# Column tiles for the adaLN products, rope tables loaded in place, and the output projection's split moved into the z stage of a hybrid backbone kernel

## The chip, the core and the metric

The kernel runs on one core of a Trainium2 chip. The metric is the device time of one execution in microseconds. The core has five engines that run their own instruction streams and meet at semaphores: TensorE (PE, matrix products; its weight loads are shown as PEld), VectorE (DVE), ScalarE (ACT), GpSimd (POOL) and SyncE (SP, which here issues nearly all DMAs). Each takes its instructions in order, so an instruction that waits holds back all that stand behind it on its engine.

## What is computed

Two layers of a diffusion backbone with 2048 latent and 256 context tokens of width 1024. Each layer modulates its input with an adaLN shift and scale, projects it once to 2560 columns, runs three mixers (a gated MLP over chunks of 128 positions, attention with rotary position codes, a recurrent scan), and projects back with w_o:

```python
shift, scale, gate = jnp.split(jax.nn.silu(c) @ w_ada + b_ada, 3, -1)
z = (x * (1 + scale[:, None]) + shift[:, None]) @ w_in
...
q = axial_rope(rms_norm(q.reshape(Bn, L, N_HEADS, HEAD_DIM), q_norm_g), rows, cols)
k = axial_rope(rms_norm(k.reshape(Bn, L, N_KV_HEADS, HEAD_DIM), k_norm_g), rows, cols)
...
attn = blocked_attention(q, jnp.concatenate([k, kc], 1), jnp.concatenate([v, vc], 1))
...
y = jnp.concatenate([mix_a * jax.nn.silu(a_g), attn * jax.nn.silu(b_g),
                     lru * jax.nn.silu(r_g)], -1) @ w_o
x_new = layer_norm(ALPHA * x + gate[:, None] * y, ln_g, ln_b)
```

The context tokens go through the same weights with their own modulation (c_ctx), read only themselves, and are not needed after the second layer's keys, values and scan states.

## The kernel before

**Numbers.** Products that need more than f16 are made of halves: a weight w becomes wh (w in f16, on ACT or POOL) and wl (the rest in f16, on DVE), an input becomes xh and xl, and PE sums xh·wh, xh·wl and xl·wh. One 128x512 split of a weight so costs one ACT and one DVE instruction.

**Stages.** The program starts with the adaLN vectors that layer 0 needs at once (shift and scale); then each layer has a z stage (0 and 1), which makes the projections and all that attention and the scans read, and an attention stage, which makes scores, softmax, the output projection and the layer norm. In the profile z stage 0 lasts to about 694 us, its attention stage to 1540, z stage 1 to 2105, and the second attention stage to the end.

**The z stage** goes over nine blocks of 256 tokens (block 0 is the context). In a block, PE runs sections: cc (the columns of the scan and its gate, transposed, `conv_in`), then the row-wise sections ag, kv, uv and bg, each as two tiles of 128 tokens of 24 matmuls of 512 columns (`nat`, L531 to L533; accumulator zps). The order of PE's instructions is written out by hand: the program is one text in which side work is woven in by `pump`, which advances a generator by a step. The order of the other four engines is set by the tile scheduler from the dependencies, and each of their queues is then fixed.

**adaLN side work.** `ada_rest` is such a generator, advanced by `pump(rest, 1)`, once in each cc product and in each tile of `nat` at k == 4: 12 visits a block from block 1 of layer 0 on. It makes the gates of layer 0 and the whole adaLN vectors of layer 1: eight rows of 512 columns, each a sum over eight chunks of w_ada (128x512, 256 KB, loaded into wga). A visit makes the two products of the chunk whose halves were made before (L376, L377: the stationary operand is vs, 128x4, which holds both halves of both condition vectors; the moving operand is the chunk's half) and then splits the next chunk (ACT L384, DVE L385) into the one buffer wgh. The four rows of the accumulator gtp are summed by a product with sel in `fin`.

**Rope.** For each tile of a latent block `rp` (the cosines and sines of its 128 tokens, 64 KB) is loaded by SP (L605); POOL multiplies it with the norm weights into ct (L607) and sn (L609). DVE multiplies the normed q and k with ct (L614), POOL multiplies the swapped halves with sn into t2 (L620, four instructions a tile), DVE adds (L622) and splits the result into kc and qc (L624 to L630). PE transposes those (kp L642, L643, qp L649), and ACT copies the transposes out to KK, KB and QS (L644, L645, L650). rp, ct, sn, t1 and t2 have one buffer each.

**The attention stage** is ordered by hand on PE, DVE, ACT and POOL, with a running count of each engine's planned time (`use(DV, 0.6)`) by which some steps choose between DVE and POOL; side work advances at set rates. `wo_prep` is its first side work: it loads w_o in eight chunks of 128x1024 and splits them into OH (ACT L915) and OL (DVE L919, two a chunk), and between them loads the gates and norm weights. Scores are sps (L975), their maxima pm (DVE L977), P is the softmax numerator, Pl its low half (L1069, on POOL or DVE); the output projection reads OH and OL at L1179 to L1181.

## Time and profile before

| | before |
|---|---|
| median of 3 runs | 2934.22 us (2933.54 to 2934.83) |
| profiled run | 2931.81 us, span 2929.8 us |
| granted TensorE clock, mean | 0.982 |
| PE, DVE, ACT, POOL busy | 93%, 71%, 48%, 61% of the span |

The profile is one execution of the program. Busy time is the time in which an engine executes; idle time of an engine is given to what it waited for last. A PE row's time includes its pipeline, so that matmuls of 0.38 us start every 0.22 us; costs on PE are therefore read from starts.

### The profile page before, as it was taken

To read this page: it belongs to the slowest core of one execution; us is meant where nothing else is said; L and a number is where in the kernel's file an instruction comes from. 1 tells how busy PE (TensorE), PEld (TensorE's weight loads), DVE (VectorE), ACT (ScalarE), POOL (GpSimd) and SP (SyncE) were. 2 spreads that over 40 slices of the span, in tenths; PEclk is the share of its full clock that TensorE was granted. 3 is DMA by queue.
4 is the path that set the end of the run, shared out by engine and by line. 5 is a ranking of instruction groups with operands and counts; after the bars stand their busy time and mean duration, and the time that the engine had idled before them with its cause. 6 is when DMAs were issued, how large, how long until landed. Compare 5 with 4: busy or idle time off the path is not lost. (4 is left out here: it accounts for less than half of the span.)

```text
span 2929.8 us, 60697 instructions
## 1 busy us (share of the span) xinstructions
PE 2735.1 (93%) x23931; PEld 1820.6 (62%) x23931; DVE 2071.7 (71%) x4102; ACT 1401.6 (48%) x2595; POOL 1782.4 (61%) x1821
## 2 busy tenths in 40 slices
PE   7999999998799999999999899999788999999998
PEld 3544454545677777677765555555466777777775
DVE  8666565558988777777877555554798877777775
ACT  5444444535554445445542454444564544544452
POOL 3233333346888877677764244433597877887775
PEclk9999999999999999999999999999999999999999
DMA  8222222105422110212115111111332210111001
GB/s 291 83 92 92 86 91 78 53 31 174 127 74 64 56 41 27 69 37 70 52 32 160 52 60 50 54 64 42 109 129 95 73 45 24 50 50 42 26 27 44
DMA packets 118255, 213.60 MB, mean 73 GB/s; under 512 B 13873, under 2 KB 45429, under 8 KB 117969
## 3 DMA queue, kind: packets, MB, share of 16 engines
q1 hardware_dynamic: 115620, 208.84, 21.8%
q8 instruction: 187, 3.06, 0.4%
q10 hardware_dynamic: 2348, 0.89, 0.1%
q14 instruction: 100, 0.81, 0.1%
HBM read 147.54 MB, written 62.14 MB: 72 GB/s over the span
## 5 line engine op out<-in xcount | busy, mean ns | idle before, releaser
L1069 POOL TENSOR_TENSOR Pl<-P 128x512 f16<-128x512 f32 x1131 | 1223.7, 1099 | 321.3 <-ACT P L1062 312.9
L1062 ACT ACTIVATE P<-stp 128x512 f32<-128x512 f32 x1160 | 692.4, 597 | 784.1 <-PE stp L1059 699.0
L977 DVE TENSOR_REDUCE pm<-sps 128x1 f32<-128x256 f32 (+1 forms) x1276 | 750.5, 625 | 270.5 <-PE sps L975 267.7
L1059 PE MATMUL stp<-aQB,KB 65*128 65x256 f16 x2320 | 582.5, 276 | 2.8 <-ACT aQB L990 2.8
L1058 PE MATMUL stp<-aQS,KK 128*128 128x256 f16 x2320 | 580.1, 275 | 3.7 <-ACT P L1062 3.2
L1086 PE MATMUL pv<-VX,P 128*128 128x129 f16 x4640 | 560.6, 220 | 0.0
L1088 PE MATMUL pv<-VX,Pl 128*128 128x65 f16 x4640 | 528.5, 193 | 6.4 <-DVE Pl L1069 3.3
L975 PE MATMUL sps<-KK,aQS 128*128 128x256 f16 (+1 forms) x1276 | 458.0, 360 | 62.2 <-DVE pm L977 59.2
L1088 PEld LDWEIGHTS <-Pl 128*128 128x128 f16 x4640 | 416.4, 98 | 99.9 <-POOL Pl L1069 5.0
L1086 PEld LDWEIGHTS <-P 128*128 128x128 bf16 x4640 | 431.1, 98 | 66.3 <-issue 51.4
L1059 PEld LDWEIGHTS <-KB 65*128 65x128 f16 x2320 | 228.7, 99 | 96.4 <-issue 5.8
L1058 PEld LDWEIGHTS <-KK 128*128 128x128 f16 x2320 | 230.6, 99 | 84.2 <-issue 14.5
L520 POOL TENSOR_SCALAR xh<-xm 128x512 f16<-128x512 f32 x68 | 45.9, 674 | 276.9 <-ACT xm L517 276.4
L531 PEld LDWEIGHTS <-xh 128*128 128x128 f16 x1040 | 102.7, 99 | 150.3 <-issue 47.4
L533 PEld LDWEIGHTS <-xl 128*128 128x128 f16 x1040 | 102.9, 99 | 124.6 <-issue 6.2
L532 PEld LDWEIGHTS <-xh 128*128 128x128 f16 x1040 | 102.8, 99 | 108.2 <-issue 4.8
L433 POOL TENSOR_SCALAR gt<-gt,sp 128x256 f32<-128x256 f32 x72 | 41.9, 591 | 199.1 <-ACT gt L430 193.2
L686 PE MATMUL cps<-xl,wh_cc 128*128 128x256 f16 x528 | 147.1, 279 | 2.7 <-DVE xl L521 2.7
L687 PE MATMUL cps<-xh,wl_cc 128*128 128x256 f16 x528 | 147.0, 278 | 1.7 <-DVE wl_cc L185 1.7
L685 PE MATMUL cps<-xh,wh_cc 128*128 128x256 f16 x528 | 147.4, 279 | 0.0
L975 PEld LDWEIGHTS <-aQS 128*128 128x128 f16 x1276 | 125.1, 98 | 11.8 <-issue 0.9
L760 ACT ACTIVATE uv<-uv 128x512 f32<-128x512 f32 x34 | 21.4, 630 | 213.0 <-DVE uv L759 213.0
(285 smaller groups left out, 5586.9 us busy)
## 6 DMA issues: line engine op xcount, KB each, us to landing
wf<-in_w_in_dram SPq DMA_DIRECT2D x64, 256.0 KB
wga<-in_w_ada_dram SPq DMA_DIRECT2D x64, 256.0 KB
lr<-LRd SPq DMA_DIRECT2D x32, 512.0 KB
SBd<-sbg SPq DMA_DIRECT2D x34, 256.0 KB
QSd<-QS SPq DMA_DIRECT2D x17, 512.0 KB
LRd<-gt SPq DMA_DIRECT2D x34, 256.0 KB
aQS<-QSd SPq DMA_DIRECT2D x17, 512.0 KB
asb<-SBd SPq DMA_DIRECT2D x17, 512.0 KB
```

What stands on the lines that cost most here:

```text
L533: T.matmul(ps[:, :w], xl[:, k, ts], wh[:, k, c0:], start=False, stop=(k == KC - 1))
L685: T.matmul(ps, wh[:, k, cs], xh[:, k], start=(k == 0), stop=False)
L686: T.matmul(ps, wh[:, k, cs], xl[:, k], start=False, stop=False)
L687: T.matmul(ps, wl[:, k, cs], xh[:, k], start=False, stop=(k == KC - 1))
L975: T.matmul(ps[:, :w], QS[:, h, t * 128:(t + 1) * 128], KK[:, kv].rearrange("p a b -> p (a b)")[:, k0:k0 + w], start=True, stop=True)
L977: V.tensor_reduce(pm[:, i:i + 1], ps[:, :w], axis=AX, op=OP.max)
L1058: T.matmul(ps[:, i], KK[:, kv, kt], QS[:, h], start=True, stop=False)
L1059: T.matmul(ps[:, i], KB[:, kv, kt], QB[:, h], start=False, stop=True)
L1062: S.activation(P, ps, AF.Exp)
L1069: less_busy(0.6, 1.04, 2.0).tensor_tensor(Pl, P, Ph, op=OP.subtract)
L1086: T.matmul(pv[:, t, 0:129], Ph[:, i, ts], VX[:, kt, kv, 0:129], start=first, stop=False, skip_group_check=True)
L1088: T.matmul(pv[:, t, 64:129], Pl[:, i, ts], VX[:, kt, kv, 64:129], start=False, stop=end, skip_group_check=True)
```

## The change

**Products.** The chunks are taken in pairs. A visit's splits fill half of a wgh of four parts (hi and lo of chunk k, hi and lo of chunk k+1); when both chunks are there, four products go to four groups of rows of one accumulator, rows 0 to 3, 32 to 35, 64 to 67 and 96 to 99, that is to four column positions of the array. The accumulator is first set to zero by a product of zeros over all 128 rows (L394), once in each of the eight sums, and sel (now 128x2) adds all four groups. A pair takes three visits: split, split, and the products with the next pair's first split. The visits stand at k == 1 and k == 5 of each tile of `nat` but the first of uv: 18 a block.

**Output projection.** The 16 tiles (128x512) of w_o of a layer are split in its z stage as further items of `ada_rest`, two visits each, and stored with f16 halves to wo_d in DRAM: in layer 0 between the gates' sums and layer 1's, in layer 1 from its third block on. The attention stage loads OH and OL from wo_d in 16 DMAs.

**Rope.** rp is gone: cosines and sines are loaded straight into ct and sn (each twice, for q's and k's half), and POOL multiplies in place.

```diff
-    sel = cst.tile([4, 2], F32, name="sel")
+    sel = cst.tile([128, 2], F32, name="sel")
...
+    wo_d = [dr.tile([KC, 2, 128, 2, 512], F16, name=f"wo_d{l}") for l in range(DEPTH)]
...
-            V.tensor_tensor(sel, idF[0:4, 0:2], idF[0:4, 2:4], op=OP.add)
+            V.tensor_tensor(sel, idF[:, 0:2], idF[:, 2:4], op=OP.add)
+            for g in range(1, 4):
+                for s in range(2):
+                    V.tensor_tensor(sel, sel, idF[:, 32 * g + 2 * s:32 * g + 2 * s + 2], op=OP.add)
...
+                if l == 0:
+                    todo = [(0, 2, 0), (0, 2, 1), None] + [(a, b, h) for a in range(1, DEPTH) for b in (2, 1, 0) for h in range(2)]
+                else:
+                    todo = [None]
...
+                def split(w):
+                    f = ws.pop(0)
+                    S.activation(w[:, 0], f, AF.Copy, scale=WS)
+                    V.scalar_tensor_tensor(w[:, 1], f, WS, w[:, 0], op0=OP.mult, op1=OP.subtract)
...
-                        if k == 0:
-                            acc = pp.tile([4, 512], F32, name="gtp", tag="zps", bufs=4)
-                        if k == 2:
-                            row = bias(l2, j, h)
-                        T.matmul(acc, vs[:, k], w[:, 0], start=(k == 0), stop=False)
-                        T.matmul(acc, vs[:, k], w[:, 1], start=False, stop=(k == KC - 1))
...
+                            acc = pp.tile([128, 512], F32, name="gtp", tag="zps", bufs=4)
+                            T.matmul(acc, zer, mov, start=True, stop=False, skip_group_check=True)
...
+                        for g in range(4):
+                            T.matmul(acc[32 * g:32 * g + 4], vs[:, k + g // 2], w[:, g], start=False,
+                                     stop=(k == KC - 2), skip_group_check=True)
...
+                        w = zp.tile([128, 2 if l else 4, 512], F16, name="wgh", tag="wgh")
+                        split(w[:, 0:2])
+                        ld(i + 1)
+                        i += 1
+                        yield
+                        if it[0] == "wo":
+                            nc.sync.dma_start(wo_d[l][it[1], it[2]], w[:, 0:2])
+                        else:
+                            split(w[:, 2:4])
                             ld(i + 1)
+                            i += 1
+                            pend = w, it
+                            yield
+                    yield
...
-                    if k == 4:
+                    if side_work and k % 4 == 1:
                         pump(rest, 1)
...
-                        rp = zp.tile([128, 2, 64], F32, name="rp", tag="rp")
-                        nc.sync.dma_start(rp, rope[r0:r0 + 128])
...
-                        G.tensor_tensor(ct, rp[:, 0:1].to_broadcast([128, 2, 64]), K.gqk, op=OP.mult)
...
+                        for a in range(2):
+                            nc.sync.dma_start(ct[:, a], rope[r0:r0 + 128, 0])
+                            nc.sync.dma_start(sn[:, a], rope[r0:r0 + 128, 1])
+                        G.tensor_tensor(ct, ct, K.gqk, op=OP.mult)
+                        G.tensor_tensor(sn, sn, K.gsw.rearrange("p a h s f -> p a (h s f)"), op=OP.mult)
...
-                        ps = nat(xTb, t, "uv")
+                        ps = nat(xTb, t, "uv", 0, t == 1)
...
-                    if l == 0 and bi == 1:
+                    if bi == (2 if last else 1):
                         rest.append(ada_rest())
...
-                    S.activation(OH[:, k], wfs[k], AF.Copy, scale=WS)
-                    yield
-                    for q in range(2):
-                        qs = slice(q * 512, (q + 1) * 512)
-                        V.scalar_tensor_tensor(OL[:, k, qs], wfs[k][:, qs], WS, OH[:, k, qs], op0=OP.mult, op1=OP.subtract)
-                        use(DV, 0.6)
-                        yield
...
+                for hl, o in ((0, OH), (1, OL)):
+                    for k in range(KC):
+                        nc.sync.dma_start(o[:, k].rearrange("p (h n) -> p h n", h=2),
+                                          wo_d[l][k, :, :, hl].rearrange("h p n -> p h n"))
```

The queues change at three places. The rows are instructions in the order in which an engine takes them, outputs left of the arrow; the numbers only tell buffers apart.

PE, block 4 of layer 0, where it takes split weights in the second uv tile; before:

```order
L533 LDWEIGHTS xl_2677
L533 MATMUL zps_3818<-wh_uv_614,xl_2677 128x512
L376 LDWEIGHTS vs_63
L376 MATMUL gtp_3616<-wgh_3800,vs_63 4x512
L377 LDWEIGHTS vs_63
L377 MATMUL gtp_3616<-wgh_3800,vs_63 4x512
L531 LDWEIGHTS xh_2676
L531 MATMUL zps_3818<-wh_uv_614,xh_2676 128x512
```

and after, in the first bg tile:

```order
L563 LDWEIGHTS xl_2662
L563 MATMUL zps_3807<-wh_bg_749,xl_2662 128x512
L400 LDWEIGHTS vs_63
L400 MATMUL gtp_3469<-wgh_3756,vs_63 4x512
L400 LDWEIGHTS vs_63
L400 MATMUL gtp_3469<-wgh_3756,vs_63 4x512
L400 LDWEIGHTS vs_63
L400 MATMUL gtp_3469<-wgh_3756,vs_63 4x512
L400 LDWEIGHTS vs_63
L400 MATMUL gtp_3469<-wgh_3756,vs_63 4x512
L561 LDWEIGHTS xh_2661
L561 MATMUL zps_3807<-wh_bg_749,xh_2661 128x512
```

The visit with products has moved from the second uv tile (after 15 of its matmuls) to the first bg tile (after 18), and has four products, each with its own weight load.

DVE in the same block, from the split that this visit takes (wgh_3800) in the rope step of tile 0 to the next one in that of tile 1; before:

```order
L385 SCALAR_TENSOR_TENSOR wgh_3800<-wga_3679,wgh_3800 128x512
L622 TENSOR_TENSOR t1_3735<-t1_3735,t2_3742 128x640
L759 SCALAR_TENSOR_TENSOR uv_3778<-uv_3778,zps_3779 128x512
L624 CAST kc_3750<-t1_3735 128x2x128
L629 CAST qc_3753<-t1_3735 128x8x64
L625 TENSOR_TENSOR kc_3750<-t1_3735,kc_3750 128x2x64
L630 TENSOR_TENSOR qc_3753<-t1_3735,qc_3753 128x8x64
L614 TENSOR_TENSOR t1_3757<-qk1_3281,ct_3760 128x512
L614 TENSOR_TENSOR t1_3757<-qk1_3281,ct_3760 128x128
L761 SCALAR_TENSOR_TENSOR uv_3778<-uv_3778,zps_3779 128x512
L622 TENSOR_TENSOR t1_3757<-t1_3757,t2_3764 128x640
L385 SCALAR_TENSOR_TENSOR wgh_3836<-wga_3803,wgh_3836 128x512
```

and after, from the rope sum of tile 0 on:

```order
L652 TENSOR_TENSOR t1_3668<-t1_3668,t2_3677 128x640
L789 SCALAR_TENSOR_TENSOR uv_3715<-uv_3715,zps_3716 128x512
L654 CAST kc_3685<-t1_3668 128x2x128
L659 CAST qc_3688<-t1_3668 128x8x64
L655 TENSOR_TENSOR kc_3685<-t1_3668,kc_3685 128x2x64
L660 TENSOR_TENSOR qc_3688<-t1_3668,qc_3688 128x8x64
L365 SCALAR_TENSOR_TENSOR wgh_3756<-wga_3603,wgh_3756 128x512
L644 TENSOR_TENSOR t1_3692<-qk1_3234,ct_3693 128x512
L644 TENSOR_TENSOR t1_3692<-qk1_3234,ct_3693 128x128
L791 SCALAR_TENSOR_TENSOR uv_3715<-uv_3715,zps_3716 128x512
L652 TENSOR_TENSOR t1_3692<-t1_3692,t2_3701 128x640
L365 SCALAR_TENSOR_TENSOR wgh_3756<-wga_3759,wgh_3756 128x512
```

Both splits of the pair (wgh_3756) now stand behind the casts of tile 0, and the second of them behind the rope sum of tile 1 as well (L644 is the former L614, L652 the former L622, L654 to L660 the former L624 to L630, L789 and L791 the former L759 and L761).

POOL, rope step of block 4 of layer 1, from tile 0's products to tile 1's; before:

```order
L620 TENSOR_TENSOR t2_24283<-qk0_23888,sn_24281 128x16x16 x2
L620 TENSOR_TENSOR t2_24283<-qk0_23888,sn_24281 128x4x16 x2
L609 TENSOR_TENSOR sn_24303<-rp_24299,gsw_20295 128x128
L607 TENSOR_TENSOR ct_24301<-rp_24299,gqk_20014 128x128
L620 TENSOR_TENSOR t2_24305<-qk1_23889,sn_24303 128x16x16 x2
L620 TENSOR_TENSOR t2_24305<-qk1_23889,sn_24303 128x4x16 x2
```

and after (L650 is the former L620, L640 the former L609, L639 the former L607):

```order
L650 TENSOR_TENSOR t2_24481<-qk0_24084,sn_24474 128x16x16 x2
L650 TENSOR_TENSOR t2_24481<-qk0_24084,sn_24474 128x4x16 x2
L640 TENSOR_TENSOR sn_24498<-sn_24498,gsw_20386 128x128
L650 TENSOR_TENSOR t2_24505<-qk1_24085,sn_24498 128x16x16 x2
L650 TENSOR_TENSOR t2_24505<-qk1_24085,sn_24498 128x4x16 x2
L639 TENSOR_TENSOR ct_24497<-ct_24497,gqk_20102 128x128
```

sn of tile 1 is multiplied in place, in the buffer that tile 0's products read, and ct of tile 1 stands behind tile 1's products instead of ahead of them.

## Rows read from the trace of the kernel before

**Rows 1.** The page: busy us, share of the span, instructions
```profile
PE 2735.1 (93%) x23931; PEld 1820.6 (62%) x23931; DVE 2071.7 (71%) x4102; ACT 1401.6 (48%) x2595; POOL 1782.4 (61%) x1821
```

**Rows 2.** By stretch: length, busy us (instructions), granted clock, DMA share, GB/s
```profile
39.00:694.00 655.00, 610.33 (x3490) 325.98 (x3491) 404.73 (x750) 303.54 (x555) 238.64 (x274) 0.97 0.28 90
1540.00:2105.00 565.00, 525.72 (x3171) 306.06 (x3170) 338.69 (x619) 249.31 (x467) 223.48 (x265) 0.98 0.21 70
314.00:319.00 5.00, 4.94 (x12) 1.64 (x12) 4.68 (x9) 1.52 (x3) 4.84 (x8) 0.50 0.23 66
722.00:820.00 98.00, 79.28 (x950) 63.21 (x948) 94.85 (x179) 56.66 (x105) 88.27 (x80) 0.97 0.39 121
820.00:920.00 100.00, 95.90 (x1048) 71.58 (x1046) 85.66 (x174) 50.08 (x98) 87.79 (x88) 1.00 0.28 82
2131.00:2230.00 99.00, 78.82 (x941) 63.16 (x939) 95.28 (x176) 57.29 (x105) 86.47 (x79) 0.97 0.37 116
2230.00:2330.00 100.00, 96.90 (x1053) 72.78 (x1053) 84.69 (x173) 49.70 (x96) 86.07 (x87) 0.98 0.23 75
```

**Rows 3.** Tile gtp: duration ns min/median/max, first and last start
```profile
L376 PE MATMUL gtp<-wgh,vs x64: 377/378/379, 116.8 to 508.9; 128*4 128x512 f16 x64
```

**Rows 4.** Timeline of PE, one visit: start us, us, engine, line, operation
```profile
229.22 0.38 PE L532 MATMUL zps<-wl_uv,xh 128*128 128x512 f16 x1
229.44 0.38 PE L533 MATMUL zps<-wh_uv,xl 128*128 128x512 f16 x1
229.75 0.38 PE L376 MATMUL gtp<-wgh,vs 128*4 128x512 f16 x1
229.96 0.38 PE L377 MATMUL gtp<-wgh,vs 128*4 128x512 f16 x1
230.27 0.39 PE L531 MATMUL zps<-wh_uv,xh 128*128 128x512 f16 x1
```

**Rows 5.** Waits by cause, 39 to 694 us: us in total, times, longest
```profile
PE gtp L377 <- DVE wgh L385: 21.4, 5, 5.0
```

**Rows 6.** Timeline of PE, second uv tile of block 4
```profile
309.17 0.38 PE L376 MATMUL gtp<-wgh,vs 128*4 128x512 f16 x1
314.06 0.58 PE L377 MATMUL gtp<-wgh,vs 128*4 128x512 f16 x1 [4.51 <-DVE wgh L385]
```

**Rows 7.** Timeline of POOL, rope products of tile 0 in block 4
```profile
310.75 3.43 POOL L620 TENSOR_TENSOR t<-qk,sn 128x256 f32<-128x256 f32 x4 [0.94 <-DVE qk L596]
```

**Rows 8.** Timeline of DVE, tile 1 of block 4
```profile
322.71 0.67 DVE L385 SCALAR_TENSOR_TENSOR wgh<-wga,wgh 128x512 f16<-128x512 f32 x1
```

**Rows 9.** Timeline of POOL, a plain block of z stage 1
```profile
1885.19 3.06 POOL L620 TENSOR_TENSOR t<-qk,sn 128x256 f32<-128x256 f32 x4 [0.94 <-DVE qk L596]
1888.32 1.09 POOL L609 TENSOR_TENSOR sn<-rp,gsw 128x128 f32<-128x128 f32 x1
1889.38 0.45 POOL L607 TENSOR_TENSOR ct<-rp,gqk 128x128 f32<-128x128 f32 x1
1889.79 2.71 POOL L620 TENSOR_TENSOR t<-qk,sn 128x256 f32<-128x256 f32 x4
```

**Rows 10.** Timeline of DVE in the same block
```profile
1892.42 1.16 DVE L614 TENSOR_TENSOR t<-qk,ct 128x512 f32<-128x512 f32 x2
```

**Rows 11.** Waits by cause, 1540 to 2105 us
```profile
PE kp L642 <- ACT KB L645: 10.2, 7, 5.9
```

**Rows 12.** Timeline of SyncE's queue, head of z stage 1
```profile
1613.21 0.80 SPq L496 DMA_DIRECT2D xn<-x_d  x2
```

**Rows 13.** Timeline of PE at the same place
```profile
1616.65 1.45 PE L514 MATMUL tr<-idF,xn 128*128 128x128 f32 x4 [7.09 <-DMA xn<-x_d]
```

**Rows 14.** Lines of ACT's and DVE's w_o split: duration ns min/median/max
```profile
L915 ACT ACTIVATE OH<-wof x16: 1047/1048/1050, 720.3 to 2213.2; 128x1024 f16<-128x1024 f32 x16
...
L919 DVE SCALAR_TENSOR_TENSOR OL<-wof,OH x32: 678/1242/1529, 722.4 to 2226.8; 128x512 f16<-128x512 f32 x32
```

**Rows 15.** Waits of PE by cause, 694 to 830 us
```profile
PE sps L975 <- DVE pm L977: 15.4, 12, 2.6
```

More of the change, by code (lines that the diff above doesn't have):

```diff
@@ L129, in turn @@
                 for k in range(KC):
-                    T.matmul(tp[:, k], rows[j][:, k // 4, k % 4 * 128:(k % 4 + 1) * 128], sel, start=True, stop=True)
+                    T.matmul(tp[:, k], rows[j][:, k // 4, k % 4 * 128:(k % 4 + 1) * 128], sel[0:4], start=True, stop=True)
                 tps.append(tp)
@@ L333, in ada_rest @@
             def ada_rest():
-                items = [(l2, j, h, k) for l2, j in [(0, 2)] + [(a, b) for a in range(1, DEPTH) for b in (2, 1, 0)]
-                         for h in range(2) for k in range(KC)]
-                ws, parts, acc, row, fins = [], [], None, None, None
+                if l == 0:
+                    todo = [(0, 2, 0), (0, 2, 1), None] + [(a, b, h) for a in range(1, DEPTH) for b in (2, 1, 0) for h in range(2)]
+                else:
+                    todo = [None]
+                items = []
+                for g in todo:
+                    if g is None:
+                        items += [("wo", k, h) for k in range(KC) for h in range(2)]
+                    else:
+                        items += [g + (k,) for k in range(KC)]
+                ws = []
                 def ld(i):
-                    l2, j, h, k = items[i]
+                    if i >= len(items):
+                        return
                     ws.append(zp.tile([128, 512], F32, name="wga", tag="xm", bufs=2))
-                    c0 = j * D + h * 512
-                    nc.sync.dma_start(ws[-1], w_ada[l2, k * 128:(k + 1) * 128, c0:c0 + 512])
-                def bias(l2, j, h):
-                    row = zp.tile([4, 512], F32, name="grow", tag="grow")
-                    V.memset(row, 0.0)
-                    c0 = j * D + h * 512
-                    nc.sync.dma_start(row[0:2], rows_bcast(b_ada[l2, c0:c0 + 512], 512, 2))
-                    return row
+                    if items[i][0] == "wo":
+                        _, k, h = items[i]
+                        src = w_o[l, k * 128:(k + 1) * 128, h * 512:(h + 1) * 512]
+                    else:
+                        l2, j, h, k = items[i]
+                        src = w_ada[l2, k * 128:(k + 1) * 128, j * D + h * 512:j * D + (h + 1) * 512]
+                    nc.sync.dma_start(ws[-1], src)
+                def split(w):
+                    f = ws.pop(0)
+                    S.activation(w[:, 0], f, AF.Copy, scale=WS)
+                    V.scalar_tensor_tensor(w[:, 1], f, WS, w[:, 0], op0=OP.mult, op1=OP.subtract)
                 def fin(l2, j, h, row):
@@ L361, in fin @@
                         nc.sync.dma_start(gate_d[l2][:, h * 512:(h + 1) * 512], row[0:2])
+                zer = MZ[1][:, 0, 0:1].to_broadcast([128, 128])
+                mov = MZ[2][:, 0:1, 0:64].to_broadcast([128, 8, 64])
+                pend, fins, acc, row = None, None, None, None
                 ld(0)
                 yield
-                for i in range(len(items) + 1):
+                i = 0
+                while i < len(items) or pend or fins:
                     if fins:
@@ L381, in ada_rest @@
                     if i < len(items):
[L382 to L387 removed]
+                        it = items[i]
+                        w = zp.tile([128, 2 if l else 4, 512], F16, name="wgh", tag="wgh")
[5 more added lines that the diff above has]
+                            nc.sync.dma_start(wo_d[l][it[1], it[2]], w[:, 0:2])
+                        else:
+                            split(w[:, 2:4])
                             ld(i + 1)
+                            i += 1
+                            pend = w, it
+                            yield
                     yield
[L390 removed]
             W = Wt[l]
@@ L522, in prep, with nat @@
                 xT[b] = (xh, xl)
-            def nat(xT_b, t, g, c0=0):
+            def nat(xT_b, t, g, c0=0, side_work=True):
                 xh, xl = xT_b
```

50 lines of the change are left out of this document (17 added, 33 removed).

## The prediction, made before the changed kernel had run

> **What bounds the kernel now.** I read the busy table first: TensorE (PE) is busy 2735.1 of 2929.8 us [rows 1], so what counts is what PE executes or waits for, and another engine matters only where PE waits for it. The table by stretches says which stage has what limit [rows 2]. In the two z stages PE is busy 93% of the time and VectorE (DVE) about 60%: PE runs the hand-written order there, and short waits break it. The first 98 us of each attention stage in which w_o is split are different: DVE is busy 94.85 of 98 us, PE only 79.28, and 100 us later PE is back at 95.90 of 100. DVE is the bound there. The change touches three places: the adaLN products in z stage 0, the rope step of every z block, and the w_o split.
>
> **Products in column tiles.** Before, 64 chunks take two matmuls each, one visit a chunk (64 first ones in [rows 3]). In the trace of one visit [rows 4] the starts stand 0.31, 0.21 and 0.31 us apart, where neighbours stand 0.22: a visit costs 0.83 − 0.22 = 0.61 us, 64 of them 39.2 us. After, 32 visits have four matmuls each in four column positions, and 8 zeroing matmuls of 0.22 us are new (1.8 us). No row shows column tiles side by side. If they stream beside each other, a visit costs one stream with its two edges, 0.31 + 0.31 − 0.22 = 0.40 us; if in a row, 0.31 + 3 × 0.21 + 0.31 − 0.22 = 1.03 us. I take 0.50, near the first, since the second matmul's weight load of rows 4 did not widen its 0.21 us. That is 16.0 + 1.8 = 17.8 us: **−21.4 us**, ends −24.6 and −4.5.
>
> The 0.31 us edges of rows 4 are what the Trainium skill, TensorEngine Tiling (Array Packing), Tiling Modes, describes: a change of tiling mode drains TensorE. Its page TensorE: Matmul & The Clock Gate, Part 3, says that a pack takes one matmul and about 4 ns for each further tile; an estimate from that is 0.41 us a visit and a sum lower by 3 us. The same part has a rule against this change: a weight load overlaps running matmuls only where its row group differs, and these four have the same rows. By it the four would go in a row, the third rival below; the 0.21 us of rows 4 speaks against it for one column position.
>
> **Waits for the split weights.** Before, PE waited five times, 21.4 us in all, for DVE's half of a chunk [rows 5], 4.51 us of it in the second uv tile of block 4 [rows 6]. In the 5 us behind that wait the granted clock is 0.50, the 1.2 GHz level, and PE makes 12 matmuls [rows 2] that at its usual step of 0.22 us would take 2.6: 2.4 us more. Five times 4.3 + 2.4 is 34 us. The cause is DVE's queue: the split stands behind the rope step, which waits for GpSimd (POOL). After, uv tile 0 has no visit, and the order of DVE puts the pair's second split behind the rope step of tile 1 (blocks 4 to 7 alike); PE wants it in the first bg tile, after 18 of its 24 matmuls. Worked from block 4: POOL ends tile 0's products at 310.75 + 3.43 = 314.2 [rows 7]; only then may the sn load be issued into the one buffer; 1.9 us to land (below), 1.1 for sn, 2.7 for tile 1's products and 0.45 for ct [rows 9], which now stands last, make 320.35; DVE then needs 1.16 for L614 [rows 10], 0.67 for the split [rows 8] and about as much for each of the two rows between: 323.5. PE, at 309.17 after 15 of uv tile 1's matmuls, has 9 + 18 left (5.8 us) and gets there at about 315. The wait is 8.5 us, with the slow matmuls behind it 11. Four blocks make 44, and I allow 5 in block 1, where a pair is only half shifted: 49 for 34, **+15 us**. Ends: −14 if the loads land at once and the waits stay at four of 5 us, +30 if all six blocks with pairs pay 10.5.
>
> **Rope tables.** Before, rp for the next tile lay ready: in a plain block POOL goes from tile 0's products straight to sn, ct and tile 1's products [rows 9]. After, ct and sn are one buffer each and are loaded themselves, so the load of sn for tile 1 waits for POOL's last read of tile 0, and SyncE issues four loads a tile in place of one. In the block of rows 9: products end 1885.19 + 3.06 = 1888.25; landing 1.9 gives 1890.15, sn 1.09 gives 1891.24, products 2.71 give 1893.95, ct 0.45 gives 1894.4. DVE started L614 of tile 1 at 1892.42 [rows 10]; it is **2.0 us later**. Behind it on DVE stand L761 of uv tile 0 and L759 of uv tile 1; ACT's second uv activation (L760) waits for the latter, and ACT's copies KK and KB stand behind that on ACT. PE's kp waits for KB already now, seven times in z stage 1, 10.2 us in all with one of 5.9 [rows 11]: there is no slack, and the 2.0 us go on to PE. The landing time is the unknown: a 256 KB load issued at 1613.21 [rows 12] released PE at 1616.65 [rows 13], so below 3.4 us; two issues of 0.40 each [rows 12] are the least, 0.8. I take 1.9, between them, since a half's load is small (32 KB). The delay is then 2.0, with ends 0.9 and 3.5. Eight blocks of z stage 1: +16 (7 to 28). At its head SyncE's queue has the next block's sn and ct loads ahead of the x load for which PE waits 7.09 us [rows 13]; the ct load waits for DVE's L614 of tile 1, about 1.3 us later than the x load's issue now: +1.3 (0 to 4). In z stage 0 blocks 2, 3 and 8 have no late pair and pay 2.0 each: +6 (3 to 10); in blocks 4 to 7 it is inside the 8.5. Together **+23 us**.
>
> **Output projection.** Before, ACT splits 16 tiles of 1.048 us and DVE 32 of about 1.2 us [rows 14], 17 and 38 us, in the two stretches of rows 2 where DVE is the bound and PE waits for DVE's maxima: 15.4 us in the first [rows 15]. After, the attention stage loads the halves ready-made, 16 loads of 256 KB, as many bytes as before, needed late (the first output projection comes after the first scores). If PE reaches its next level at once, layer 0 gains 98 × (0.959 − 0.809) = 14.7 us and layer 1 99 × (0.969 − 0.796) = 17.1: 32 at best. If DVE fills the room with other due work, the share of the split in its time there (19 of 95) of the 19 and 20 us lost: 8 at least. I take 13 a layer, a little under the 15.4 us of waits: **−26 us**. The 16 splits a layer move to the z stages: 0.67 us each on DVE [rows 8], 11 us in about two blocks, where DVE is 60% busy; PE needs none of their results, so only what stands behind them on DVE pays, and the store, for which the next item's one wgh buffer waits, sits in SyncE's queue. 0 to 6 us, I take **+2**. The six additions for sel at the start are tiny and hidden behind the first loads; the bias load at k = 0 is earlier than before: nothing.
>
> **How the numbers follow.** −21.4 + 15 + 23 − 26 + 2 = −7.4 us on the profiled run's 2931.8: 2924.4. The median of before is 2.4 us above that run, so I say **2927 us** for the median. The ends of the terms do not add up in one direction; about ±13 us around it are likely.
>
> **Rivals.**
> - *The loads are early enough* (chance 0.22). The landing is short, and what PE waited for in rows 11 had another last cause than this chain, so that DVE's delay ends before PE: the rope terms fall to +5, the pair waits stay at 34. −21.4 + 0 + 5 − 26 + 2 = −40: **2893**. For it: DVE is only 60% busy in these stages [rows 2]. Against it: the chain of rows 9 to 11 has no slack, and the buffer is single.
> - *The single buffer costs more than the rest brings* (0.25): slower. Place: sn of tile 1 in every block. At the end of 3.5 us a block, z stage 1 pays 28 + 4, blocks 2, 3 and 8 pay 10, four waits are longer by 1.5 (+21 in place of +15): −21.4 + 21 + 42 − 26 + 2 = +18: **2952**. It decides from about 0.5 us more a block: 15 blocks × 0.5 = 7.5 us cancel the forecast's gain.
> - *The column tiles go in a row* (0.13): 32 × 1.03 + 1.8 = 34.8 for 39.2, the sum +10: **2944**. For it: the page's rule above; against it: rows 4.
> - The forecast, 0.40.
>
> About 0.2% (5.9 us, so 2928.3 and 2940.1) is what a measurement can tell from no change. The forecast lies close to the first of these: I give it 0.24 faster, 0.14 the same, 0.02 slower. The early loads are 0.22 faster; the single buffer 0.05 the same and 0.20 slower; the row of tiles 0.01 faster, 0.04 the same, 0.08 slower. Together 0.47, 0.23 and 0.30. The range, 2888 to 2953, takes in the rivals' centres and leaves out only their far ends; the forecast's own is 2914 to 2940.
>
> **What would show it.** Right: starts within a visit of four matmuls a few hundredths apart; PE's wait for the split weights (now on the four-matmul line) four or five times near 8.5 us in the first bg tile; DVE's L614 of tile 1 (a later line number) waiting for POOL's ct; PE's kp waits in z stage 1 two us longer a block; z stage 0 about as long as now, z stage 1 about 19 us longer, DVE no longer 97% busy at the head of the attention stages and each stage 13 us shorter. Wrong: starts 0.21 us apart (tiles in a row); sn for tile 1 standing on POOL without a gap behind the products (loads early); a rope delay of 3 us or more; or attention stages unchanged because PE was held by the maxima anyway.

## The result: slower by 0.87%

| | before | changed |
|---|---|---|
| median | 2934.15 us (2933.54 to 2934.83) | 2959.61 us (2959.04 to 2961.6) |
| profiled run's span | 2929.8 us | 2957.6 us |
| granted clock, mean | 0.982 | 0.972 |

The ratio is 1.0087 (95% interval 1.0074 to 1.01), +25.5 us; the forecast was 2927. The page's busy table of the changed kernel, beside [rows 1]:

```profile
PE 2729.9 (92%) x23939; PEld 1829.9 (62%) x23939; DVE 2055.8 (70%) x4113; ACT 1400.5 (47%) x2611; POOL 1761.8 (60%) x1816
```

PE is busy 5 us less than before and the span is 28 us longer. By stages, each counted from PE's first cc product of a layer or its first scores to the next such point (start: until layer 0's first cc product; attention 1: until PE's last product):

| us | start | z stage 0 | attention 0 | z stage 1 | attention 1 |
|---|---|---|---|---|---|
| before | 39.5 | 654.4 | 843.2 | 567.6 | 815.9 |
| changed | 41.5 | 670.3 | 839.6 | 593.8 | 803.2 |
| difference | +2.0 | +15.9 | −3.6 | +26.2 | −12.7 |
| forecast | 0 | +1 | −13 | +18 | −13 |

The same view by stretches as [rows 2], of the changed kernel: the z stages, then the heads of the attention stages and the 100 us behind them (length, busy us and instructions by engine, granted clock, DMA share, GB/s):

```profile
41.50:711.80 670.30, 595.59 (x3496) 331.01 (x3494) 405.12 (x765) 307.74 (x570) 232.26 (x272) 0.94 0.31 101
1551.30:2145.10 593.80, 541.21 (x3188) 314.35 (x3187) 336.00 (x641) 259.10 (x484) 218.59 (x267) 0.96 0.25 84
740.00:838.00 98.00, 88.30 (x1072) 70.42 (x1070) 91.23 (x182) 54.90 (x108) 88.94 (x85) 1.00 0.33 107
838.00:938.00 100.00, 92.38 (x995) 68.80 (x992) 87.99 (x168) 47.74 (x93) 85.80 (x86) 0.98 0.25 79
2171.00:2270.00 99.00, 89.24 (x1078) 70.96 (x1075) 92.98 (x186) 55.26 (x108) 90.48 (x86) 1.00 0.34 111
2270.00:2370.00 100.00, 95.42 (x1053) 71.42 (x1052) 84.46 (x168) 49.88 (x96) 87.19 (x87) 1.00 0.21 67
```

z stage 1, which has no adaLN products at all, is the largest loss. The same row for the whole of it before:

```profile
1537.10:2104.70 567.60, 528.32 (x3188) 307.54 (x3186) 340.96 (x624) 250.81 (x468) 224.10 (x266) 0.98 0.21 71
```

Of its 26.2 us, 13.3 are idle time of PE (593.80 − 541.21 for 567.60 − 528.32). The other 12.9 are busy time: PE takes 541.21 us in place of 528.32 for the same 3188 products, since its granted clock fell from 0.98 to 0.96. In z stage 0 the clock fell from 0.97 to 0.94, and PE's idle time grew by 30 us.

At the heads of the attention stages PE is busy 88.30 and 89.24 us where it was 79.28 and 78.82 [rows 2]: 9 and 10 us are gained there. Its wait for the maxima in the first stage's head, 15.4 us in [rows 15], is now:

```profile
PE sps L990 <- DVE pm L992: 8.3, 9, 1.9
```

Layer 1 keeps the gain. Layer 0 does not: in the 100 us behind the head PE is busy 92.38 us, before 95.90. From there to the end of the stage its waits for the maxima are 18.5 us (14.4 before), those for DVE's r, the sum ahead of the layer norm, 5.6 (2.1 before).

**Column tiles.** PE's timeline of one visit, beside [rows 4] (start us, us, engine, line, operation):

```profile
362.22 0.38 PE L562 MATMUL zps<-wl_kv,xh 128*128 128x512 f16 x1
362.44 0.38 PE L563 MATMUL zps<-wh_kv,xl 128*128 128x512 f16 x1
362.75 0.39 PE L400 MATMUL gtp<-wgh,vs 128*4 128x512 f16 x4
363.07 0.39 PE L561 MATMUL zps<-wh_kv,xh 128*128 128x512 f16 x1
```

The four products start 3 to 4 ns apart (x4 in one row), each with a weight load of its own, and take one stream's time: the next full-width matmul starts 0.32 us behind the first of them. The visit costs 0.31 + 0.32 − 0.22 = 0.41 us.

**The rope step.** The block of z stage 1 that answers to [rows 9], on POOL:

```profile
1915.98 3.06 POOL L650 TENSOR_TENSOR t<-qk,sn 128x256 f32<-128x256 f32 x4 [0.94 <-DVE qk L626]
1921.35 0.81 POOL L640 TENSOR_TENSOR sn<-sn,gsw 128x128 f32<-128x128 f32 x1 [2.30 <-DVE kc L655]
1922.24 1.97 POOL L650 TENSOR_TENSOR t<-qk,sn 128x256 f32<-128x256 f32 x4
1924.17 0.46 POOL L639 TENSOR_TENSOR ct<-ct,gqk 128x128 f32<-128x128 f32 x1
```

its loads on SyncE's queue (issues, not landings):

```profile
1919.07 0.81 SPq L638 DMA_DIRECT2D sn<-in_rope_dram  x2
1919.98 0.85 SPq L637 DMA_DIRECT2D ct<-in_rope_dram  x2
```

and DVE's step from tile 0 to tile 1, which stands in [rows 10] for before:

```profile
1921.16 0.68 DVE L660 TENSOR_TENSOR qc<-t,qc 128x512 f16<-128x512 f32 x1
1924.66 0.90 DVE L644 TENSOR_TENSOR t<-qk,ct 128x512 f32<-128x512 f32 x2 [2.81 <-POOL ct L639]
```

POOL ended tile 0's products at 1919.04, SyncE issued sn at once, the multiplication began at 1921.35 when both halves had landed (2.28 us from the first issue), ct came last, and DVE waited 2.81 us for it. The row of the multiplication names DVE's kc, which ended 0.1 us earlier; in the plain blocks it begins 2.2 to 2.5 us behind the first issue, whether kc or the load is named, so the load is what it waits for. All of z stage 1, waits by cause (us in total, times, longest), beside [rows 11]:

```profile
PE kp L672 <- ACT KB L675: 28.7, 7, 9.3
...
POOL sn L640 <- DMA sn<-in_rope_dram: 23.3, 12, 2.6
...
DVE t L644 <- POOL ct L639: 18.7, 7, 2.8
```

PE's wait for KB went from 10.2 to 28.7 us. In a plain block, one without w_o pieces, PE waits 3.4 us in all, before 2.3 us; the block takes 65.2 us for 62.5. The rest of the 2.7 us is the clock. The wait for KB ends the block, and these are the first 5 us of the next one, before and after (behind the length PE's busy time and, in brackets, its matmuls; the granted clock stands third from the end):

```profile
1837.80:1842.80 5.00, 5.00 (x50) 4.47 (x48) 1.55 (x4) 1.80 (x4) 3.73 (x4) 1.00 0.13 52
1867.10:1872.10 5.00, 5.00 (x35) 3.86 (x33) 1.50 (x4) 1.84 (x5) 3.78 (x4) 0.66 0.13 52
```

Behind a wait of 0.7 us the granted clock stayed at 1.00; behind one of 3.2 us it was 0.66, part of the stretch at the 1.2 GHz level, and PE made 35 matmuls in place of 50.

**z stage 0.** Waits by cause, beside [rows 5]:

```profile
PE gtp L400 <- DVE wgh L365: 29.6, 8, 6.5
...
ACT wgh L364 <- DMA wo_d<-wgh: 25.4, 9, 7.8
...
PE cps L715 <- ACT rx L725: 10.9, 3, 5.1
...
PE gsu L375 <- ACT KB L675: 7.9, 1, 7.9
```

The wait for DVE's half is 29.6 us in blocks 4 to 7, before 21.4 in blocks 1 to 5. In block 1, where the pairs of the gates begin, PE waits 7.9 us at the product gsu that ends a sum. The rows on the store and on rx have no counterpart before. ACT waits 25.4 us for the store of w_o pieces, whose buffer it wants for the next split, and PE waits 10.9 us for ACT's copy rx, which stands behind that split on ACT. One such place, ACT in block 4:

```profile
334.20 0.63 ACT L364 ACTIVATE wgh<-wga 128x512 f16<-128x512 f32 x1 [7.78 <-DMA wo_d<-wgh]
...
336.64 0.64 ACT L364 ACTIVATE wgh<-wga 128x512 f16<-128x512 f32 x1
337.17 0.64 ACT L725 ACTIVATE rx<-cps 128x256 f32<-128x256 f32 x2
```

and the store on SyncE's queue:

```profile
332.14 0.33 SPq L413 DMA_DIRECT2D wo_d<-wgh  x1
```

The store was issued at 332.14, ACT's split followed 2.06 us later after 7.78 us of idling, the next split at 336.64 and rx at 337.17; PE waited 4.3 us for that rx. So the store's landing is only 2.06 of the 7.78 us. Before it the store had to wait for DVE's half of the same piece, which ended at 332.11:

```profile
331.43 0.68 DVE L365 SCALAR_TENSOR_TENSOR wgh<-wga,wgh 128x512 f16<-128x512 f32 x1
```

### The profile page after: what moved, and what is told of

It is laid out like the page before. It is cut to its first block, busy times and chain, and to the rows that moved or that the text cites. A ratio compares the mean times of both kernels' runs of the same rounds, so it can differ in the third digit from the quotient of the medians.

```text
span 2957.6 us, 61023 instructions
## 1 busy us (share of the span) xinstructions
PE 2729.9 (92%) x23939; PEld 1829.9 (62%) x23939; DVE 2055.8 (70%) x4113; ACT 1400.5 (47%) x2611; POOL 1761.8 (60%) x1816
## 5 line engine op out<-in xcount | busy, mean ns | idle before, releaser
L715 PE MATMUL cps<-xh,wh_cc 128*128 128x256 f16 x528 | 155.6, 295 | 11.9 <-ACT rx L725 11.9
L716 PE MATMUL cps<-xl,wh_cc 128*128 128x256 f16 x528 | 155.2, 294 | 3.2 <-DVE xl L551 3.2
L717 PE MATMUL cps<-xh,wl_cc 128*128 128x256 f16 x528 | 154.2, 292 | 0.7 <-DVE wl_cc L189 0.7
L790 ACT ACTIVATE uv<-uv 128x512 f32<-128x512 f32 x34 | 21.4, 630 | 226.8 <-DVE uv L789 226.8
```

Source lines behind the costliest of these rows:

```text
L715: T.matmul(ps, wh[:, k, cs], xh[:, k], start=(k == 0), stop=False)
L716: T.matmul(ps, wh[:, k, cs], xl[:, k], start=False, stop=False)
L717: T.matmul(ps, wl[:, k, cs], xh[:, k], start=False, stop=(k == KC - 1))
```

## The experiments

All ratios are against the kernel before on the same chip, whose medians there were 2933.0 to 2935.2. Stage lengths are counted as above, from each kernel's profiled execution. Where a kernel's code in layer 1 is that of before, z stage 1 has between 567.6 and 571.7 us (four such kernels), and the start varies from 38.7 to 45.7 with the same code; smaller differences are not read. In z stage 1 the context's block is short (13.9 us) and stands second; below, the second block length is that block and the next one together, and the w_o pieces begin in it.

### The rope part alone, and with two buffers

```diff
 (kernel before, with the change's rope lines; one buffer, then two)
-                        ct = zp.tile([128, 2, 64], F32, name="ct", tag="ct")
-                        sn = zp.tile([128, 2, 64], F32, name="sn", tag="sn")
+                        ct = zp.tile([128, 2, 64], F32, name="ct", tag="ct", bufs=2)
+                        sn = zp.tile([128, 2, 64], F32, name="sn", tag="sn", bufs=2)
```

> The kernel before with the rope part of the change alone (cosines and sines loaded straight into the single buffers of ct and sn). Theory 1, the single buffer: tile 1's tables are loaded only after tile 0's products, 2.2 to 2.8 us a block in the 16 blocks with rope, all of it on PE's path: 2934 + 16 x 2.5 = about 2974 us, z stage 1 longer by 20 to 24. Theory 2, the w_o pieces in the z stages cost the time and the rope step next to nothing: 2934 to 2940.

> The same with two buffers each for ct and sn, so that the loads need not wait for tile 0's products. Theory 1 (the buffer): the cost goes, 2931 to 2940 us. Rival (the four small loads a tile and their place in SyncE's queue cost, not the buffer): stays near the kernel with one buffer, 2965 or more.

Rope alone, with single buffers: 2964.76 us, ratio 1.0099 (1.0083 to 1.0116), z stage 0 +13.3 and z stage 1 +16.3. With two buffers: 2936.64 us, 1.0011 (1.0001 to 1.002). The waits of PE in z stage 1, first of the single buffer, then of two:

```profile
PE kp L642 <- ACT KB L645: 26.7, 7, 6.0
```

```profile
PE kp L642 <- ACT KB L645: 11.1, 6, 5.7
```

With two buffers POOL multiplies the next tables behind tile 1's products:

```profile
1887.96 3.06 POOL L620 TENSOR_TENSOR t<-qk,sn 128x256 f32<-128x256 f32 x4 [0.94 <-DVE qk L596]
1892.02 2.26 POOL L620 TENSOR_TENSOR t<-qk,sn 128x256 f32<-128x256 f32 x4 [1.00 <-DVE t L622]
1894.24 0.90 POOL L610 TENSOR_TENSOR sn<-sn,gsw 128x128 f32<-128x128 f32 x1
1895.10 0.91 POOL L609 TENSOR_TENSOR ct<-ct,gqk 128x128 f32<-128x128 f32 x1
```

So the single buffer is the cost, 28 of 31 us; the four small loads and their places in SyncE's queue leave about 3. Theory 1 had the place and was too dear, 40 us for 31.5. The rope part by itself loses more than the whole change does.

### The changed kernel with the prefetch back in layer 1

```diff
 (changed kernel)
-                        items += [("wo", k, h) for k in range(KC) for h in range(2)]
+                        items += [("wo", k, c, n) for k in range(KC) for c, n in (((0, 384), (384, 384), (768, 256)) if l else ((0, 512), (512, 512)))]
...
+                        if l:
+                            rp = zp.tile([128, 2, 64], F32, name="rp", tag="rp")
...
+                            nc.sync.dma_start(rp, rope[r0:r0 + 128])
```

> The changed kernel with the prefetched rope table back in layer 1 only; to make room its w_o pieces in layer 1 are 384, 384 and 256 columns wide, 24 of them for 16. Theory 1: z stage 1 gives back 20 to 24 of its 26 us: 2959.6 - 22 = about 2938 us. Theory 2 (w_o pieces): z stage 1 stays within 6 us of the changed kernel, 2953 to 2962, or grows with the eight more pieces.

2951.47 us, 1.0058 (1.0039 to 1.0076); z stage 1 is 581.1 us, 12.7 shorter than in the changed kernel. Its plain blocks without w_o pieces are back at 62.5 us, as before (65.2 in the changed kernel). 13.5 us stay over the kernel before, most of them in the first three block lengths (96.0, 83.4 and 70.0 us for 91.8, 82.2 and 64.2) and at its end (35.2 for 33.7). Theory 1 holds for the blocks without pieces, but it was asked to explain the whole stage and explains half. The other half is w_o's, here with 24 pieces in place of 16.

### The changed kernel without the move of w_o

```diff
 (changed kernel)
-                    todo = [(0, 2, 0), (0, 2, 1), None] + [(a, b, h) for a in range(1, DEPTH) for b in (2, 1, 0) for h in range(2)]
+                    todo = [(0, 2, 0), (0, 2, 1)] + [(a, b, h) for a in range(1, DEPTH) for b in (2, 1, 0) for h in range(2)]
...
+                    S.activation(OH[:, k], wfs[k], AF.Copy, scale=WS)
```

> The changed kernel with the old w_o split in the attention stages. If the move of w_o is worth its attention gain (16 us) and costs nothing in the z stages: 2976 us. If the pieces cost PE about as much in the z stages (waits of ACT for the store of the one buffer, 10 us in z stage 0, 4 in z stage 1): 2958 to 2964.

2945.11 us, 1.0037 (1.0025 to 1.0049): faster than the changed kernel by some 14 us, outside both expectations. Without the move z stage 0 is 650.5 us (670.3 with it), z stage 1 582.9 (593.8), the attention stages 843.3 and 813.8 (839.6 and 803.2). The move gains 3.7 and 10.6 us and costs 19.8 and 10.9. PE runs as many products in the z stages with the move as without; of the 30.7 us that it costs, 17 are idle time of PE and 13 are products at the lower clock (PE is busy 595.59 us for 587.64 in z stage 0, 541.21 for 535.94 in z stage 1).

The gain in layer 0 is small beside the scatter. Kernels that split w_o in attention stage 0 have 840.8 to 845.0 us there, the three that load it 839.3 to 843.9. In attention stage 1 the two groups stand apart: 812.6 to 815.9 in ten kernels, 803.2 to 807.8 in five, 8.5 us between the means.

Against the rope part alone (2964.76), this kernel has the column tiles and the pairs besides: they are worth 19.7 us.

### The move of w_o in layer 1 alone

```diff
 (kernel before; wo_rest makes 24 pieces, two visits each)
+                    if last and bi == 2:
+                        rest.append(wo_rest())
...
-    backs, preps, later = [lru_back(lrp)], [wo_prep()], ...
+    backs, preps, later = [lru_back(lrp)], [wo_load() if l else wo_prep()], ...
```

> The kernel before with the w_o split of layer 1 alone moved into z stage 1, in 24 pieces of at most 384 columns, two visits each; rope, products and layer 0 as before. Theory 3 (the pieces cost PE in the z stage about what the attention stage gains): attention stage 1 shorter by 11 to 13 us, z stage 1 longer by 8 to 11: 2930 to 2936 in all. Rival (only rope made z stage 1 longer): 2922, z stage 1 within 2 us of before.

2943.05 us, 1.0036 (1.0023 to 1.0049). Attention stage 1 is 10.6 us shorter, z stage 1 19.0 longer (15 than the longest with unchanged code). Theory 3 had the sign and was too kind in size; the rival is out.

### Which part of a piece costs

Four edits take the pieces apart:

```diff
 (a third visit behind each piece, changed kernel)
                             nc.sync.dma_start(wo_d[l][it[1], it[2]], w[:, 0:2])
+                            yield
 (layer 0's pieces without their store, attention stage 0 splits w_o itself)
+                            if l:
                             nc.sync.dma_start(wo_d[l][it[1], it[2]], w[:, 0:2])
 (empty visits in place of layer 0's pieces, w_o split in the attention stages)
+                    if i < len(items) and items[i][0] == "wo":
+                        i += 1
...
+                        yield
 (kernel before, layer 1's pieces split in z stage 1 without store, unused)
-                    nc.sync.dma_start(wo_d[l][k, :, :, c:c + n], wt)
```

> The changed kernel with a third, empty visit behind each w_o piece, so that the store of the one wgh buffer has time to land before the next split. Theory 4 (ACT waits 25 us in z stage 0 for that store, and the scan's rx copy that PE needs stands behind it on ACT): the waits of PE's cc products for rx go (11 us), 2948 to 2952 from 2959.6. Rival (the pieces cost because they push the adaLN pairs into two more blocks, each with its wait of 8 us): no better or worse, 2959 to 2968.

2956.79 us, 1.0074 (1.0052 to 1.0096). z stage 0 is 662.6, 7.7 shorter, but ACT's waits for the store are still 20.2 us (25.4) and PE's for rx 9.0 (10.9): the visit did not give the store time, so this run does not tell the theories apart. A store goes when DVE's half is done, as at 332.11 above, and a visit more on PE does not bring that forward.

> The changed kernel with layer 0's w_o pieces split but not stored and attention stage 0 splitting w_o as before; layer 1 as in the changed kernel. Theory 4: z stage 0 shorter by 8 to 12 us (no wait of ACT for the store, none of PE's cc products for rx), attention stage 0 longer by 4: 2950 to 2955. Rival (the pieces' visits push the pairs into two more blocks): z stage 0 stays near 670, in all 2960 to 2965.

2956.28 us, 1.0071 (1.0055 to 1.0087), a little above the range of theory 4. z stage 0 is 660.8 us, 9.5 shorter, attention stage 0 3.7 longer. Its waits of PE in z stage 0:

```profile
PE gtp L400 <- DVE wgh L365: 29.1, 8, 6.1
...
PE cps L716 <- ACT rx L726: 0.8, 2, 0.7
```

The wait for rx is gone (0.8 for 10.9), the other is not. Theory 4 holds in layer 0. Whether a second wgh buffer would save as much was not run.

> The changed kernel with the old w_o split in both attention stages, and in layer 0, where the changed kernel has its 32 visits for w_o, as many empty ones: no load, no split, no store. Theory 6 (the pieces' visits cost by pushing the adaLN pairs into two more blocks, each with its wait of about 8 us): z stage 0 near 660 us against 650.5 without them, in all about 2955. Rival (an empty visit costs nothing, the rest of the pieces' cost is their splits on ACT and DVE): z stage 0 650 to 653, 2943 to 2948.

2948.4 us, 1.005 (1.0034 to 1.0067); z stage 0 is 651.8 us for 650.5 without the visits. An empty visit costs next to nothing in z stage 0, although the pairs' waits do move into later blocks: each block with pairs has one stretch of waiting, wherever the block stands, and those that they left are free of it (65.5 and 63.7 us in blocks 2 and 3 for 73.3 and 73.9, 72.5 and 74.9 in blocks 6 and 7 for 64.9 and 64.1). The medians of the two kernels differ by 3 us, with intervals that overlap. Theory 6 falls. In z stage 0 a move of w_o so costs 1.3 us for the visits, 9.0 for the loads and splits and 9.5 for the stores (651.8, 660.8, 670.3).

> The kernel before with layer 1's 24 w_o pieces split in z stage 1 but not stored, their results unused; the attention stages split w_o as before. Theory 4 (the store, for which the one buffer and ACT wait): z stage 1 longer by at most 5 us, where the same pieces with their store made it 19 us longer: 2934 to 2939. Rival (the splits' own place in the queues of ACT and DVE, and the room that their buffer takes): z stage 1 longer by 14 to 20 again, 2947 to 2953, since the attention stage gains nothing here.

2948.42 us, 1.0044 (1.0028 to 1.0059); z stage 1 is 582.2, 14.6 longer than in the profile of before (10.5 than the longest with unchanged code), and 4.4 shorter than with the store. In layer 1 the rival holds: the splits cost, the store little. But 7 us of it lie in the first two block lengths (94.8 and 86.3; 91.8 and 82.2 before). In the second, from 1636.2 on, the first pieces are split. ACT and DVE wait for the first one's load, and that split stands on DVE ahead of the scan's steps on which PE waits:

```profile
1641.52 0.52 ACT L407 ACTIVATE wgo<-wga 128x384 f16<-128x384 f32 x1 [2.06 <-DMA wga<-in_w_o_dram]
1642.08 0.56 DVE L408 SCALAR_TENSOR_TENSOR wgo<-wga,wgo 128x384 f16<-128x384 f32 x1 [2.17 <-ACT wgo L407]
1647.48 0.28 PE L443 MATMUL gps<-xrh,lwh 128*128 128x256 f16 x1 [2.54 <-DVE xrh L430]
```

Before, PE did not wait for xrh there. With a longer wait for KB at the end of this length (7.3 us for 5.9) that is its 4 us.

> The kernel before with only two w_o pieces in layer 1, in its last block, not stored and unused: the buffer is there, the work is not. Theory 7 (half of the 14.6 us that 24 split pieces cost in z stage 1 comes from the buffer's room and the queue order that the scheduler then chooses, since the first two blocks, which have no piece, are 7 us longer): those two blocks 5 to 7 us longer than before, 2939 to 2942. Rival (it is the pieces' work alone): z stage 1 within 2 us of before, 2933 to 2936.

```diff
 (the kernel of wo1_split_no_store, two pieces in place of 24)
-                    if last and bi == 2:
+                    if last and bi == NB - 1:
```

2937.9 us, 1.001 (1.0001 to 1.0019), between the two expectations; z stage 1 is 574.3. Its first block is 96.0 us (91.8 before), its second length 82.3 as before. PE's wait for the context's load in the first block, between 1537 and 2111 us:

```profile
PE tr L535 <- DMA xn<-c_d: 6.6, 2, 5.9
```

before it was 1.4 us in the same stage. SyncE's queue shows why. These are the issues of that load, in the kernel before and in this one:

```profile
1576.39 0.90 SPq L496 DMA_DIRECT2D xn<-c_d  x2
1581.72 0.90 SPq L517 DMA_DIRECT2D xn<-c_d  x2
```

Before, it goes 39.3 us into the stage, behind 11 loads of weights (wf); here 44.9 us into it, behind 15. This holds for every kernel: the seven with the pieces' buffer in layer 1 issue it at 44.0 to 44.9 us, wait 5.6 to 6.6 us and have a first block of 94.8 to 97.2 us; the eight without have 39.0 to 40.0, 0.7 to 1.7 and 91.2 to 93.7. So the buffer alone, by the order that the scheduler then gives the queue, costs about 3 us there, and theory 7 holds in part, for the first block. The second length's 4 us are the pieces' work, as the rows above show.

### The wait for split weights, and two column tiles

```diff
 (kernel before)
-                        ps = nat(xTb, t, "uv")
+                        ps = nat(xTb, t, "uv", 0, t == 0)   # no visit in the second uv tile
...
 (two column tiles)
-                        T.matmul(acc, vs[:, k], w[:, 0], start=(k == 0), stop=False)
-                        T.matmul(acc, vs[:, k], w[:, 1], start=False, stop=(k == KC - 1))
+                        for g in range(2):
+                            T.matmul(acc[32 * g:32 * g + 4], vs[:, k], w[:, g], start=False, stop=(k == KC - 1),
+                                     skip_group_check=True)
```

> The kernel before without the adaLN visit in the second uv tile, where PE waits for DVE's half, 11 visits a block for 12. Theory 5 (the five waits of 4.3 us and the slow clock behind them are costs of that place alone): about 2934 - 34 + 3 = 2903 us. Rival (the next visit, in the first bg tile, waits as long for the split behind tile 1's rope step): 2925 to 2940.

2941.89 us, 1.0029 (1.0017 to 1.0041): slower. The waits of PE in z stage 0:

```profile
PE gtp L377 <- DVE wgh L385: 8.7, 6, 2.6
PE zps L531 <- DVE uv L761: 6.1, 5, 1.2
PE qp L649 <- DVE adaT L356: 5.7, 1, 5.7
```

The wait for the split is 8.7 us for 21.4, but PE now waits for the next things that DVE owes: the accumulators that DVE's uv step frees, and adaT. So the waits moved more than they went; theory 5 falls. With 11 visits a block the side work also lasts longer: its last product is at 550.9 us for 509.1, and blocks 6 and 7 take 73.5 and 66.4 us for 66.5 and 62.5. How much of the loss is this and how much the moved waits, no run here separates.

> The same, and the two products of a chunk in two column positions of one accumulator, with one zeroing product a sum. If column tiles stream beside each other here as the four do in the changed kernel (starts 3 ns apart), each of the 64 visits costs 0.21 us less and the eight zeroing products 0.22 each more: 11 to 12 us below the kernel without that visit. If what the visits cost is the waits alone: no difference over 3 us.

2930.44 us, 0.9992 (0.9983 to 1.0001), 11.5 us below the kernel without that visit, as expected of tiles beside each other.

> The kernel before with the two products of each chunk in two column positions of one accumulator and nothing else; the visits, the rope step and w_o as before. Column tiles beside each other: 64 x 0.21 us less, 8 x 0.22 more, 11 to 12 us faster than before, 2921 to 2923. If the waits for DVE's half, now reached earlier, take it back: 2930 to 2934.

2925.69 us, 0.9965 (0.9951 to 0.9979): 9.1 us faster than the kernel before, a little less than the 11 to 12 of the tiles' own sum, and the fastest of all runs. Its visit on PE:

```profile
221.08 0.38 PE L539 MATMUL zps<-wh_kv,xl 128*128 128x512 f16 x1
221.39 0.38 PE L382 MATMUL gtp<-wgh,vs 128*4 128x512 f16 x2
221.70 0.39 PE L537 MATMUL zps<-wh_kv,xh 128*128 128x512 f16 x1
```

## Why the prediction was wrong

**The products: right.** The tiles stream beside each other; a visit costs 0.41 us where I took 0.50, so 32 × 0.41 + 1.8 = 14.9 for 39.2, −24.3 for −21.4. On the chip the tiles and pairs were worth 19.7 us (after_without_wo against rope_only), in which longer waits are taken off already. The third rival is out. The Trainium skill's rule that spoke for it (TensorE: Matmul & The Clock Gate, Part 3: weight loads overlap running matmuls only if row groups differ) does not hold for these four, which share their rows and start 3 to 4 ns apart. The pack rule of the same part of the Trainium skill, one matmul and about 4 ns a tile, gave an estimate of 0.41, which is what the trace shows.

**The waits for split weights: near in size.** I had 8.5 us each in the first bg tile of blocks 4 to 7. PE's timeline of block 5:

```profile
459.26 0.38 PE L563 MATMUL zps<-wh_bg,xl 128*128 128x512 f16 x1
459.57 0.38 PE L400 MATMUL gtp<-wgh,vs 128*4 128x512 f16 x1
465.44 0.59 PE L400 MATMUL gtp<-wgh,vs 128*4 128x512 f16 x2 [5.49 <-DVE wgh L365]
468.12 0.58 PE L400 MATMUL gtp<-wgh,vs 128*4 128x512 f16 x1 [2.10 <-DVE wgh L365]
```

From 459.57 over the first split to the second is 5.87 us, and 2.7 more before the fourth product: 8.5 us from the first product to the last. The four blocks have 7.7, 8.5, 7.7 and 9.1; the idle time in them is 29.6 us, 7.4 a block. The 5 us that I allowed in block 1 were 7.9.

**The rope step: right in mechanism, near in size in part by luck.** I had 2.0 us a block from a landing of 1.9. The landing took 2.28, but DVE was idle meanwhile, and with DVE idle POOL made tile 1's products in 1.97 us (2.71 beside a busy DVE [rows 9]); DVE's L644 took 0.90, alone, for 1.16 [rows 10]. So L644 starts 5.6 us behind the end of tile 0's products where it started 4.2 behind it: 1.4 us later, not 2.0. The block still grew by 2.7 us, because the clock fell behind PE's wait, a price that I had put on the pair waits and left out here: 1.1 us of the 2.7 are waits, the rest is products at the lower clock. A delay put too high and a clock put at nothing nearly cancel. The part alone cost 31.5 us; I had 23 and most of the waits' 15.

**These terms together** were −21.4 + 15 + 23 = +16.6; the changed kernel without the move of w_o measured +11.9 (2945.11 for 2933.26). The forecast failed elsewhere.

**The output projection: wrong, and this turned the sign.** The step that failed is the price of the move: −26 us for the attention stages and +2 for the z stages. Measured (with and without the move): −14.3 and +30.7. Two sizes were wrong.
- The gain: layer 1 gave 10.6 of my 13, layer 0 only 3.7. In layer 1 it is 8.5 between the means of all kernels. In layer 0 the head did gain 9 us (PE's busy time 88.30 for 79.28 of 98 us), and some 5 of them were lost behind it, in longer waits for the maxima and for r (18.5 and 5.6 us for 14.4 and 2.1). That the planner's counts of other engines' time, which the change alters, order the work worse there is a guess; no run tests it.
- The cost: I reckoned 11 us of DVE per layer, "PE needs none of their results", and so let it hide in an engine that is 60% busy. PE needs what stands behind them. In z stage 0 the loads and splits cost 9.0 us and the stores 9.5, the latter through one wgh buffer: ACT waits for DVE's half and for the store behind it, and rx for ACT. I had named that store and the queue, and priced both with 0 to 6 us. In z stage 1 the splits, the buffer's effect on the first block and the stores came to 11 us in the changed kernel and 15 to 19 on the kernel before. Some 13 of the 30.7 us of both stages are the lower clock behind the added waits, for which my term had nothing. The split's 0.63 and 0.67 us sit in front of a chain (rope, uv, KB) on which PE was already waiting, as I had argued for the rope step itself [rows 11]; the same argument applied to any work put on these queues in these stages.

**The rival that came nearest** was the slower one, the single buffer at 2952, with 0.25. Its mechanism is there in every block, but not at its price: without its two w_o terms its sum is −21.4 + 21 + 42 = +41.6, and without the move the kernel measured +11.9. That 2952 lies nearest to the result is luck; the rest of the loss is w_o's. The range ended at 2953, because the term of w_o had no end above +6 −8 = −2 us: its gain was bounded on both sides from rows, its cost in the z stages by a guess.

What stays open: why attention stage 0 gives back most of what its head gains.

## What to carry to other kernels

An engine that is 60% busy is no cover if its queue carries the chain on which the bound engine waits: price added work there at its full length first, and then look for slack in the waits. A wait of PE can cost more than its length: here products behind it ran at the lower clock, and in a plain block that was more than the wait had grown by. A move of work pays only by the difference of two stages, so both ends need the same care; here one of the two stages that were relieved gave back most of its gain, and those that were loaded had no room. The table that is computed in place here needed a second buffer once its load came from memory (28 of 31 us), and small products with four rows each cost 3 to 4 ns more when they stood in other columns beside a first.

## What the runs showed that was not expected

Four 128x4 by 512 products with weight loads of their own start 3 to 4 ns apart in four column positions and cost PE 0.41 us together, one stream with its two edges. A store of 256 KB freed its buffer 2.06 us after its issue (332.14 to 334.20; up to 3.5 elsewhere), and a load of two halves of 32 KB reached its reader 2.28 us after its first issue. POOL's rope products of tile 1 took 1.97 us with DVE idle and 2.7 with DVE busy. A buffer that is used only in a stage's last block made that stage's first block about 3 us longer, through the order of SyncE's queue at its head. Half of what z stage 1 lost is no wait at all: the same products, at a granted clock of 0.96 in place of 0.98.
